# One-pass products read and write backwards, with token tiles at sixteen starting places

## The chip, the cores and the metric

The kernel runs on one core of a Trainium2 chip. The metric is the device time of one execution in microseconds. The median of three runs stands for a kernel, and one more execution is profiled.

## What is computed

The reference is a trunk of two layers for 512 tokens of width 1024, in float32. Tokens are mixed by differential attention in the first layer and by chunked gated linear attention in the second; in both, four heads attend to 256 memory tokens beside it. One input projection feeds all heads, one output projection takes their joined results, and a gated MLP with a causal convolution of width 3 follows. Cut to its skeleton:

```
for i in range(2):
    h = rms_norm(x, attn_norm[i])
    proj = h @ w_in                                  # one input projection
    mix = diff_attention(proj) if i == 0 else gla_attention(proj)
    cross = memory_cross_attention(proj, mem)        # 4 heads, 256 memory tokens
    x = x + concatenate([mix, cross]) @ w_out[i]
    h = rms_norm(x, ffn_norm[i])
    u = causal_conv(h @ w_up[i]) + conv_b[i]
    a, g = split(u)
    x = x + (silu(g) * a) @ w_down[i]
```

Nearly all of the arithmetic is in the products with `w_in`, `w_mem_kv`, `w_out`, `w_up` and `w_down`.

## The kernel before

The residual stream is kept transposed: eight tiles `xT[k]` of 128 features by 512 tokens. Two such tiles share one buffer of 4096 bytes a partition (`x2`, sixteen buffers); `pair` and `split_tiles` hand out the two halves, and `load_x` takes whole buffers.

A float32 product is made of three products in the type float32r, which TensorE runs in one pass. Each operand is split in a rounded part and the rest, `hi` on ScalarE (lines 227, 263, 306) and `lo` on VectorE (lines 230, 265, 309), and hi x hi, hi x lo and lo x hi are summed in PSUM. These are the one-pass products of the change. They stand at four places:

- `gemm` (lines 327 to 329): the input and memory projections. The stationary operand is a block of 128 tokens of an `x2` tile, the moving operand a slice of weights with 512, 272 or 256 columns.
- the first projection (line 507), of the same kind, while the inputs still arrive.
- `product` (lines 348 to 350): the output and up projections. Here the weights are stationary and the moving operand is a tile of 512 tokens.
- `down` (line 1173): the down projection, worked as a scheme of half-size blocks with fewer products. The weights are stationary and the moving operand is a block of 256 tokens, in an `x2` tile or in `midh` and `midl`, which are not of `x2`.

Attention, the transposes (`transpose`, line 196) and the sums of squares use float32, which takes several passes; they are not touched.

Weights come as blocks of 512 KB by DMA from the SP queue into six raw buffers and are split into five buffers of `whi` and five of `wlo`. The order on TensorE is that in which the program is written. In the attention layers a queue of work (`Filler`) puts a few microseconds of projection between steps of attention, and its costs and fill times are fixed numbers in the code. In the MLP each group of up projections is followed by its `down`.

Where tiles lie matters to this change. As allocated, every tile that a one-pass product of the change reads starts at 416 modulo 512 bytes: all `x2`, `whi`, `wlo`, `midh`, `midl` and the tiles of the mixers' results. Stationary slices step by 512 bytes, moving ones by 512, 1024 or 2048, so both operands of a product start at the same place modulo 512. The exception is the projection with 272 columns, whose weight slices step by 1088 bytes and start at 416, 480 and 32.

Of the kernel before, what the change touches and what calls it, by code (L numbers as in the profile page):

```python
# [11 lines left out]
F32 = mybir.dt.float32  # L12
# [9 lines left out]
S = 512  # L22
KT = D // 128
# [8 lines left out]
X2, XS, EM = 16, 5, 7  # L32
# [118 lines left out]
def trunk(ctx, tc, head_d, x_t, mem_t, wpack, cols_a_d, cols_d, conv_d, gate_d, rel_bias, diff_lambda, consts, onehot, out):  # L151
    nc = tc.nc
    mm = nc.tensor.matmul
# [3 lines left out]
    xs = ctx.enter_context(tc.tile_pool(name="xs", bufs=1))  # L157
# [6 lines left out]
    def bank(tag):  # L164
        return ps.tile([128, 512], F32, name=f"ps_{tag}", tag=tag)

    def xtile():
        return xs.tile([128, S], F32, name="xt", tag="xs", bufs=XS)

    def pair(dt=F32):  # L170
        t = xs.tile([128, 2, S], dt, name="x2", tag="x2", bufs=X2)
        return t[:, 0], t[:, 1]

    def split_tiles(pool=None, tag=None, bufs=None):
# [8 lines left out]
    def blk(b, w=128):  # L183
        return slice(w * b, w * b + w)
# [5 lines left out]
    ones = C[:, 640:768]  # L190
    eps = perm.tile([128, 1], F32, name="eps")
    V.memset(eps, EPS)

    def transpose(dst, src):
        n = src.shape[0]
        nc.tensor.transpose(dst, src, ident[:n, :n])  # L196
# [117 lines left out]
    def gemm(sh, sl, nb, key, w, evac, hook=None, order=None, hold=1):  # L314
        got, open_, held = [], {}, []
        order = order or [(b, "mm") for b in range(nb)]

        def unit(b, tag, k0, k1):
            if not got:
                for x in key if isinstance(key, list) else [key]:  # L320
                    got.extend(weights(x))
            if k0 == 0:
                open_[b] = bank(tag)[:, :w]
            p = open_[b]
            for k in range(k0, k1):
                hi, lo = got[k]
                mm(p, sh[k][:, blk(b)], hi, start=k == 0, stop=False)  # L327
                mm(p, sh[k][:, blk(b)], lo, start=False, stop=False)  # L328
                mm(p, sl[k][:, blk(b)], hi, start=False, stop=k == KT - 1)  # L329
            if k1 == KT:  # L330
                held.append(b)
                if len(held) < hold:
                    return
                if hook is not None and order[hold - 1][0] == b:
                    hook()
                for x in [x for x in held if x in open_]:
                    evac(x, open_.pop(x))
        for b, tag in order:
            for k in range(0, KT, 2):
                F.add(6 * w / 2370.0, lambda b=b, tag=tag, k=k: unit(b, tag, k, k + 2))  # L340


    def product(p, parts, n, pairs, ids=None):
        ids = range(len(parts)) if ids is None else ids
        first, last = (ids[0], ids[-1]) if len(ids) == len(parts) else (0, len(parts) - 1)
        for i in ids:
            (hi, lo), (bh, bl) = parts[i], pairs[i]
            mm(p, hi[:, blk(n)], bh, start=i == first, stop=False)  # L348
            mm(p, hi[:, blk(n)], bl, start=False, stop=False)  # L349
            mm(p, lo[:, blk(n)], bh, start=False, stop=i == last)  # L350


    xT, xpair = [None] * KT, [None] * (KT // 2)
# [56 lines left out]
    first = [bank("mm"), bank("mm"), bank("sm"), bank("sm")]  # L410
# [24 lines left out]
    with tc.tile_pool(name="ini", bufs=1) as ip, tc.manual_schedule(engines={E.Activation, E.DVE, E.Pool, E.SP}):  # L435
        idle = ip.tile([128, 512], F32, name="idle")
        rb = ip.tile([32, 6], F32, name="rb")
        oh = ip.tile([32, 640], F32, name="oh")
        bs = pair()
        bs = bs[0][:6], bs[1][:6, :128]  # L440
        lv = xtile()[:, :256]
        G.memset(idle, 0.0)
        p = bank("tp")
        for n in (512, 320):
            mm(p[:, :n], idle[:, 0:128], idle[:, :n], start=True, stop=True)


        raws = [ip.tile([128, WTILE], F32, name=f"raw{i}") for i in range(4)]
        A.dma_start(raws[0][:, blk(0, S)], wpack[0, :, blk(0, S)])
        head = ip.tile([128, 32 + S], F32, name="head")  # L450
        for c in (slice(0, 32 + S // 2), slice(32 + S // 2, 32 + S)):
            load(head[:, c], head_d[:, c])
        xT[0] = head[:, 32:]
        for k in range(1, KT):
            if k % 2:
                two = pair()
            xT[k] = two[1 - k % 2]
            load(xT[k], x_t[k])
            load(raws[k // 2][:, blk(k % 2, S)], wpack[k // 2, :, blk(k % 2, S)])
        load(cols_a, cols_a_d)  # L460
        at[0] = 4
        load(C[:, 640:768], consts[:, 640:768])
        load(rb, rel_bias)
        load(oh, onehot)
        second = [load_raw(raw_tile(), WTILE) for _ in range(3)]
        load(cols, cols_d)
        load(lv, diff_lambda[0].rearrange("a b -> (a b)").partition_broadcast(128))
        parts, acc, split_w = [], [None], [None]
        made.append(parts)

        def operands(k):
            if k % 2 == 0:
                split_w[0] = [wp.tile([128, WTILE], F32R, name=n, tag=n, bufs=WB) for n in ("whi", "wlo")]
            c = blk(k % 2, S)
            hi, lo = split_w[0]
            xh[k], xl[k] = split_tiles()
            if k == 0:
                V.tensor_copy(hi[:, c], raws[0][:, c])
                V.tensor_sub(lo[:, c], raws[0][:, c], hi[:, c].bitcast(F32))
                for t in (blk(0, S // 2), blk(1, S // 2)):  # L480
                    split(xh[0][:, t], xl[0][:, t], xT[0][:, t], col(0, head))
            else:
                split(xh[k], xl[k], xT[k], col(k, head))
                split_weights(c, raws[k // 2], hi, lo)
            parts.append((hi[:, c], lo[:, c]))
            squares(xT[k], acc)

        operands(0)
        for k in range(KT):
            if k + 1 < KT:  # L490
                operands(k + 1)
            if k == 0:
                second.append(load_raw(raws[0], WTILE))
            if k == 4:
                bias_rows(rb, oh, bs)
            if k == KT - 2:
                make_piece(second, lambda: token_rsqrt("lg", acc[0], NB, r_x[:, 0]))
                weights(("qk", 0))
                small_vectors()
                for c in range(2):  # L500
                    load(bias_d[:, 512 * c:min(512 * c + 512, 640)], bs[c])
            hi, lo = parts[k]
            terms = (xh[k], hi), (xh[k], lo), (xl[k], hi)
            todo = [(b, i) for b in range(NB) for i in range(3)]
            for b, i in sorted(todo, key=lambda bi: bi[1]) if k == 0 else todo:
                xp, w = terms[i]
                mm(first[b], xp[:, blk(b)], w, start=k == 0 and i == 0, stop=k == KT - 1 and i == 2)

    load(C[:, 0:640], consts[:, 0:640])
    for i in range(4):  # L510
# [545 lines left out]
    def load_x(src):  # L1056
        for k in range(KT):
            if k % 2 == 0:
                xpair[k // 2] = xs.tile([128, 2, S], F32, name="x2", tag="x2", bufs=X2)
            xT[k] = xpair[k // 2][:, k % 2]  # L1060
            nc.sync.dma_start(xT[k], src[k])

# [43 lines left out]
    def ffn(pool, l, acc):  # L1106
# [47 lines left out]
        def down(g, mids, finish):  # L1154
            last, ks = len(mids) - 1, tuple(range(len(mids)))
            parts, banks, first, last_group = {}, {}, used[0], g + 1 == len(GROUPS)

            def step(c, tag, w, m, ks=ks, start=False, more=True):
                if (c, w) not in parts:
                    parts[c, w] = weights(("d", l, g, c, w), more)  # L1160
                elif more:
                    prefetch(first + more)
                if start:
                    banks[c, tag] = bank(tag)
                p = banks[c, tag]
                hi, lo = parts[c, w]
                for k in ks:
                    mh, ml = mids[k][m]
                    for n in range(2):
                        o, ws = p[:, blk(n, 256)], slice(256 * k + 128 * n, 256 * k + 128 * n + 128)  # L1170
                        terms = (hi, mh), (hi, ml), (lo, mh)
                        for i, (a, b) in enumerate(terms):
                            mm(o, a[:, ws], b, start=start and (k, n, i) == (0, 0, 0), stop=k == last and i == 2,  # L1173
                               skip_group_check=True)

            def add(c, tag, f, t):
# [91 lines left out]
        for what, i in _ffn():  # L1268
            if what == "up":
# [12 lines left out]
                if i % 2 == 0:  # L1282
                    w = pool.tile([128, 8, 256], F32, name="w", bufs=1)
# [3 lines left out]
            else:  # L1287
                n, last = GROUPS[i], i == len(GROUPS) - 1
# [93 lines left out]
```

## Time and profile before

| | |
|---|---|
| median of 3 runs | 1171.81 us (1171.26 to 1171.84) |
| the profiled execution | 1170.8 us |
| its span, from first to last instruction | 1168.9 us |
| granted TensorE clock | 1.000 |
| TensorE busy | 1155.8 us, 99% of the span |
| VectorE busy | 886.6 us, 76% |
| ScalarE busy | 599.2 us, 51% |
| DMA | 117.94 MB, mean 101 GB/s |

In the profile PE is TensorE, PEld its loads of stationary operands (which lie beside its products), DVE is VectorE and ACT ScalarE. A product's row shows its length from start to finish; successive products overlap, so the time that each takes from the next is the distance between their starts.

### The profile page before, as it was taken

To read this page: it belongs to the slowest core of one execution; us is meant where nothing else is said; L and a number is where in the kernel's file an instruction comes from. 1 tells how busy PE (TensorE), PEld (TensorE's weight loads), DVE (VectorE), ACT (ScalarE), POOL (GpSimd) and SP (SyncE) were. 2 spreads that over 40 slices of the span, in tenths; PEclk is the share of its full clock that TensorE was granted. 3 is DMA by queue.
4 is the path that set the end of the run, shared out by engine and by line. 5 is a ranking of instruction groups with operands and counts; after the bars stand their busy time and mean duration, and the time that the engine had idled before them with its cause. 6 is when DMAs were issued, how large, how long until landed. Compare 5 with 4: busy or idle time off the path is not lost.

```text
span 1168.9 us, 16705 instructions
## 1 busy us (share of the span) xinstructions
PE 1155.8 (99%) x6448; PEld 988.7 (85%) x6448; DVE 886.6 (76%) x1454; ACT 599.2 (51%) x1048; POOL 4.1 (0%) x17
## 2 busy tenths in 40 slices
PE   9999999999999999999999999999999999999998
PEld 6887777788898889988998788988889988998888
DVE  7747687679886778668897746868998677876885
ACT  6856677566444444344467534536654344434441
POOL 0000000000000000000000000000000000000000
PEclk9999999999999999999999999999999999999999
DMA  9432213143225222522253221144221632253212
GB/s 313 162 97 90 68 55 127 59 129 97 64 70 182 91 73 72 162 93 70 66 169 112 73 73 46 55 153 126 86 68 64 189 99 73 72 155 98 72 37 73
DMA packets 39853, 117.94 MB, mean 101 GB/s; under 512 B 4735, under 2 KB 7608, under 8 KB 39774
## 3 DMA queue, kind: packets, MB, share of 16 engines
q1 hardware_dynamic: 39630, 116.62, 31.7%
q8 instruction: 51, 0.84, 0.3%
q14 instruction: 28, 0.23, 0.1%
q10 hardware_dynamic: 144, 0.26, 0.1%
HBM read 112.65 MB, written 4.21 MB: 100 GB/s over the span
## 4 chain that ended last, share of the span: by engine, by line
PE 91%; DVE 6%; ACT 2%; issue 1%; DMA 0%; DVEq 0%; ACTq 0%
PE ps_lg L1173 10%; PE ps_mm L348 9%; PE ps_mm L349 9%; PE ps_mm L350 9%; PE ps_sm L350 7%; PE ps_sm L348 7%; PE ps_sm L349 7%; PE ps_mm L327 5%; PE ps_mm L329 5%; PE ps_mm L328 5%; PE ps_tp L1173 5%; PE ps_mm L1173 3%; PE ps_tp L196 2%; PE ps_lg L686 1%; PE ps_sm L722 1%; DVE wlo L230 1%
## 5 line engine op out<-in xcount | busy, mean ns | idle before, releaser
L230 DVE TENSOR_TENSOR wlo<-raw,whi 128x1024 fp32r<-128x1024 f32 (+4 forms) x164 | 186.5, 1140 | 86.5 <-ACT whi L227 85.7
L227 ACT CAST whi<-raw 128x1024 fp32r<-128x1024 f32 (+4 forms) x164 | 160.7, 985 | 155.6 <-PE ps_sm L349 69.9
L348 PE MATMUL ps_mm<-x,whi 128*128 128x512 f32 x438 | 172.6, 394 | 0.3 <-DVE midh L1264 0.3
L349 PE MATMUL ps_mm<-x,whi 128*128 128x512 f32 x438 | 170.6, 389 | 0.2 <-DVE x L309 0.2
L350 PE MATMUL ps_mm<-x,wlo 128*128 128x512 f32 x438 | 170.6, 390 | 0.0
L348 PE MATMUL ps_sm<-x,whi 128*128 128x512 f32 x378 | 148.0, 392 | 0.0
L349 PE MATMUL ps_sm<-x,whi 128*128 128x512 f32 x378 | 147.1, 389 | 0.0
L350 PE MATMUL ps_sm<-x,wlo 128*128 128x512 f32 x378 | 147.1, 389 | 0.0
L327 PE MATMUL ps_mm<-whi,x 128*128 128x512 f32 (+2 forms) x336 | 132.0, 393 | 0.0
L329 PE MATMUL ps_mm<-whi,x 128*128 128x512 f32 (+2 forms) x336 | 126.6, 377 | 0.5 <-DVE x L309 0.4
L328 PE MATMUL ps_mm<-wlo,x 128*128 128x512 f32 (+2 forms) x336 | 125.9, 375 | 0.0
L263 ACT CAST whi<-raw 128x1024 fp32r<-128x1024 f32 (+1 forms) x60 | 58.3, 978 | 86.7 <-PE ps_sm L349 26.2
L348 PEld LDWEIGHTS ps_mm<-x,whi 128*128 128x128 f32 x438 | 82.3, 188 | 17.4 <-issue 0.9
L350 PEld LDWEIGHTS ps_mm<-x,wlo 128*128 128x128 f32 x438 | 82.2, 188 | 17.1
L349 PEld LDWEIGHTS ps_mm<-x,whi 128*128 128x128 f32 x438 | 82.3, 188 | 17.0 <-DVE x L309 0.6
L265 DVE TENSOR_TENSOR wlo<-raw,whi 128x1024 fp32r<-128x1024 f32 (+1 forms) x60 | 67.9, 1131 | 25.2 <-ACT whi L263 25.1
L349 PEld LDWEIGHTS ps_sm<-x,whi 128*128 128x128 f32 x378 | 71.0, 188 | 15.1 <-issue 0.5
L348 PEld LDWEIGHTS ps_sm<-x,whi 128*128 128x128 f32 x378 | 71.0, 188 | 15.0 <-issue 0.5
L350 PEld LDWEIGHTS ps_sm<-x,wlo 128*128 128x128 f32 x378 | 70.9, 188 | 14.8
L1173 PE MATMUL ps_lg<-midh,whi 128*128 128x256 f32 x264 | 75.0, 284 | 1.8 <-DVE x L1178 1.8
L1173 PE MATMUL ps_lg<-midl,whi 128*128 128x256 f32 x264 | 74.7, 283 | 0.0
L1173 PE MATMUL ps_lg<-midh,wlo 128*128 128x256 f32 x264 | 74.7, 283 | 0.0
(308 smaller groups left out, 2287.2 us busy)
## 6 DMA issues: line engine op xcount, KB each, us to landing
raw<-in_wpack_dram SPq DMA_DIRECT2D x170, 512.0 KB, 3.6
raw<-in_wpack_dram SPq DMA_DIRECT2D x24, 384.0 KB, 3.1
x<-in_x_t_dram SPq DMA_DIRECT2D x15, 256.0 KB, 5.2
xres<-x SPq DMA_DIRECT2D x8, 256.0 KB, 3.7
x<-xres SPq DMA_DIRECT2D x8, 256.0 KB, 5.1
raw<-in_wpack_dram SPq DMA_DIRECT2D x7, 256.0 KB, 5.4
bt<-bias_d SPq DMA_DIRECT2D x6, 256.0 KB, 4.9
x<-in_mem_t_dram SPq DMA_DIRECT2D x4, 256.0 KB, 6.1
```

The lines of the kernel that those rows point to most:

```text
L196: nc.tensor.transpose(dst, src, ident[:n, :n])
L227: ins = A.copy(hi[:, c], raw[:, c])
L230: V.tensor_sub(lo[:, c], raw[:, c], hi[:, c].bitcast(F32))
L263: A.copy(hi[:, c], raw[:, c])
L265: todo = [lambda: V.tensor_sub(lo[:, c], raw[:, c], hi[:, c].bitcast(F32)), lambda: [sum_weights((*key[:3], *x)) for x in after]]
L327: mm(p, sh[k][:, blk(b)], hi, start=k == 0, stop=False)
L328: mm(p, sh[k][:, blk(b)], lo, start=False, stop=False)
L329: mm(p, sl[k][:, blk(b)], hi, start=False, stop=k == KT - 1)
L348: mm(p, hi[:, blk(n)], bh, start=i == first, stop=False)
L349: mm(p, hi[:, blk(n)], bl, start=False, stop=False)
L350: mm(p, lo[:, blk(n)], bh, start=False, stop=i == last)
L1173: mm(o, a[:, ws], b, start=start and (k, n, i) == (0, 0, 0), stop=k == last and i == 2, skip_group_check=True)
```

## The change

Two things change together. A buffer of `x2` gets 32 bytes more, so the sixteen buffers, which lie one behind the other, start at sixteen places modulo 512 bytes, 32 apart (416, 448, 480, 0, 32 and so on to 384). And at the four places above, the moving operand and the output are given with step -1 along the columns, so the columns pass through TensorE in the reverse order and land where they landed before. Stationary operands are read as before, and the weight tiles and `midh`, `midl` start where they did. The four small products of line 885 stay forward.

```diff
+    def two_tiles(dt=F32):
+        t = xs.tile([128, 2 * S + 8], dt, name="x2", tag="x2", bufs=X2)
+        return t[:, :2 * S].rearrange("p (a b) -> p a b", a=2)
+
     def pair(dt=F32):
-        t = xs.tile([128, 2, S], dt, name="x2", tag="x2", bufs=X2)
+        t = two_tiles(dt)
         return t[:, 0], t[:, 1]
...
+    def back(t):
+        return t[:, ::-1]
...
-                mm(p, sh[k][:, blk(b)], hi, start=k == 0, stop=False)
-                mm(p, sh[k][:, blk(b)], lo, start=False, stop=False)
-                mm(p, sl[k][:, blk(b)], hi, start=False, stop=k == KT - 1)
+                mm(back(p), sh[k][:, blk(b)], back(hi), start=k == 0, stop=False)
+                mm(back(p), sh[k][:, blk(b)], back(lo), start=False, stop=False)
+                mm(back(p), sl[k][:, blk(b)], back(hi), start=False, stop=k == KT - 1)
...
-            mm(p, hi[:, blk(n)], bh, start=i == first, stop=False)
-            mm(p, hi[:, blk(n)], bl, start=False, stop=False)
-            mm(p, lo[:, blk(n)], bh, start=False, stop=i == last)
+            mm(back(p), hi[:, blk(n)], back(bh), start=i == first, stop=False)
+            mm(back(p), hi[:, blk(n)], back(bl), start=False, stop=False)
+            mm(back(p), lo[:, blk(n)], back(bh), start=False, stop=i == last)
...
-                mm(first[b], xp[:, blk(b)], w, start=k == 0 and i == 0, stop=k == KT - 1 and i == 2)
+                mm(back(first[b]), xp[:, blk(b)], back(w), start=k == 0 and i == 0, stop=k == KT - 1 and i == 2)
...
-                xpair[k // 2] = xs.tile([128, 2, S], F32, name="x2", tag="x2", bufs=X2)
+                xpair[k // 2] = two_tiles()
...
-                            mm(o, a[:, ws], b, start=start and (k, n, i) == (0, 0, 0), stop=k == last and i == 2,
+                            mm(back(o), a[:, ws], back(b), start=start and (k, n, i) == (0, 0, 0), stop=k == last and i == 2,
                                skip_group_check=True)
```

The order of the instructions stays the same on every engine. What the built program has besides is a wait of TensorE for its own semaphore (`PE_49`) on some first products of an accumulation. 71 of its rows name such a wait, where 55 did. One of the places is in the first layer's output projection, beside attention's products. TensorE's rows there before:

```order
L686 MATMUL ps_lg<-kT,qT 128x128 x2
L722 MATMUL ps_sm<-v_388,em 128x128 [waits Activation_49]
L722 MATMUL ps_sm<-v_388,em 128x128 x3
L348 MATMUL ps_mm<-x_1240,whi 128x512
L349 MATMUL ps_mm<-x_1240,whi 128x512
```

And with the change, where the lines of the file are 7 further down:

```order
L693 MATMUL ps_lg<-kT,qT 128x128 x2
L729 MATMUL ps_sm<-v_388,em 128x128 [waits Activation_49]
L729 MATMUL ps_sm<-v_388,em 128x128 x3
L355 MATMUL ps_mm<-x_1240,whi 128x512 [waits PE_49]
L356 MATMUL ps_mm<-x_1240,whi 128x512
```

The first product of the output projection's sum now waits for an earlier product of TensorE; nothing has changed places.

## The prediction

> **What bounds the kernel now.** I read the clock first, then the busy times and the chain of waits, then TensorE's own waits.
>
> ```profile
> core 0: 1168.9 us, clock 1.000
> PE 1155.8 (99%) x6448; PEld 988.7 (85%) x6448; DVE 886.6 (76%) x1454; ACT 599.2 (51%) x1048; POOL 4.1 (0%) x17
> PE 91%; DVE 6%; ACT 2%; issue 1%; DMA 0%; DVEq 0%; ACTq 0%
> ```
> ```profile
> PE ps_lg L1173 <- DVE x L1178: 1.8, 2, 0.9
> ...
> PE ps_mm L349 <- DVE x L309: 0.2, 1, 0.2
> ```
>
> The clock is full, TensorE is busy for 99% of the span and holds 91% of the chain, and the longest of its twelve kinds of wait adds up to 1.8 us. So the time is what TensorE takes per product times the number of products. "Busy" hides the interesting part, since products overlap (one is shown as 0.39 us long and the next starts before it ends). What counts is the distance from start to start, which the timeline of TensorE gives for 512 columns, and the merged pieces of the chain for 256:
>
> ```profile
> 399.74 0.39 PE L348 MATMUL ps_mm<-x,whi 128*128 128x512 f32 x1
> 399.96 0.39 PE L349 MATMUL ps_mm<-x,whi 128*128 128x512 f32 x1
> ...
> 402.46 0.39 PE L348 MATMUL ps_mm<-x,whi 128*128 128x512 f32 x1
> ```
> ```profile
> 463.93 8.64 PE ps_lg L1173 x72
> ```
>
> Twelve products from 399.74 to 402.46 are 226.7 ns each; 72 products in 8.64 us are 120.0 ns each. The difference of 106.7 ns for 256 columns is 0.4167 ns a column, and 226.7 - 512 x 0.4167 = 13.3 ns is left over, the same 13.3 at 256 columns (120.0 - 106.7). Every one-pass product pays these 13.3 ns besides its columns.
>
> Is that the price of changing the weights? The four-pass float32 products and the transposes change them just as often (timeline pieces, with the mean length of one from the groups by line):
>
> ```profile
> 704.66 0.81 PE L1000 MATMUL ps_sm<-gv,x 128*128 128x192 f32 x4
> L1000 PE MATMUL ps_sm<-gv,x x32: 323/324/328, 704.7 to 776.9; 128*128 128x192 f32 x32
> 151.53 1.03 PE L196 MATMUL ps_tp<-C,em 128*128 128x128 f32 x8
> L196 PE MATMUL ps_tp<-C,em 128*128 128x128 f32 x92 | 14.0, 273 | 0.0
> ```
>
> Start to start is (0.81 - 0.324)/3 = 162 ns at 192 columns and (1.03 - 0.273)/7 = 108 ns at 128: 0.84 ns a column, twice the one-pass figure, and about 2 ns left over. So a change of weights costs about 2 ns where the moving operand is read at half the speed, and 13.3 where it is read at full speed. That looks like a full-speed stream held up by something that a half-speed stream absorbs, and what runs beside every product is the load of the next weights. Two more places of the timeline say that the 13.3 is not rigid. First the products with 272 columns, whose moving operands begin at three places modulo 512 bytes, while in all other one-pass products of the kernel before both operands begin at one and the same place (so the tiles are allocated); then 512 columns in a stretch broken up by float32 work:
>
> ```profile
> 611.59 0.29 PE L327 MATMUL ps_mm<-whi,x 128*128 128x272 f32 x1
> ...
> 614.23 0.29 PE L327 MATMUL ps_mm<-whi,x 128*128 128x272 f32 x1
> ```
> ```profile
> 149.69 0.39 PE L328 MATMUL ps_mm<-wlo,x 128*128 128x512 f32 x1
> ...
> 150.84 0.39 PE L327 MATMUL ps_mm<-whi,x 128*128 128x512 f32 x1
> 151.08 0.39 PE L328 MATMUL ps_mm<-wlo,x 128*128 128x512 f32 x1
> 151.30 0.39 PE L329 MATMUL ps_mm<-whi,x 128*128 128x512 f32 x1
> ```
>
> The 21 products from 611.59 to 614.23 take 125.7 ns, 12.4 over their columns. The seven from 149.69 to 151.30 take 230 ns, and single ones 240 and 220 (the view rounds to 10 ns): the left-over moves between about 7 and 27 ns, with the same instructions. I read that as a hold-up that depends on how the two reads, of the moving operand and of the next weights, lie to each other.
>
> **The change part by part.** *Direction.* The number of products reversed comes from the windows over the whole span for lines 348 (349 and 350 are its twins), 327 (328 and 329 likewise), 507 and 1173, in this order, with the forms of 327:
>
> ```profile
> 0.00:1168.90 1168.90, 326.81 (x832) 156.23 (x832) 1.00 0.32 101
> 0.00:1168.90 1168.90, 136.69 (x352) 66.30 (x352) 1.00 0.32 101
> 0.00:1168.90 1168.90, 22.78 (x96) 17.90 (x96) 1.00 0.32 101
> 0.00:1168.90 1168.90, 223.59 (x1848) 222.75 (x1848) 1.00 0.32 101
> ```
> ```profile
> L327 PE MATMUL ps_mm<-whi,x 128*128 128x512 f32 x288 | 117.8, 409 | 0.0
> L327 PE MATMUL ps_mm<-whi,x 128*128 128x256 f32 x32 | 9.6, 301 | 0.0
> ```
>
> 3 x 832 + 3 x 352 + 96 + 1848 = 5496 products. 3456 of them have 512 columns, 3 x 32 + 1848 = 1944 have 256, and the other 96 have 272. Their left-overs are 5496 x 13.3 ns = 73 us, 6% of the span, nearly all on the path. How fast the two reads pass each other follows from the loads:
>
> ```profile
> L348 PEld LDWEIGHTS ps_mm<-x,whi 128*128 128x128 f32 x438 | 82.3, 188 | 17.4 <-issue 0.9
> ...
> L619 PEld LDWEIGHTS ps_tp<-em,vm 128*64 128x64 f32 x64 | 3.4, 136 | 1.6 <-ACT em L711 0.8 <-issue 0.5 <-ACT rs_y L217 0.3
> ```
>
> 64 columns more take 52 ns more, so a load reads its 512 bytes in about 104 ns, in which the moving operand advances by about 1024. Read in the same direction, the two places shift by 512 bytes against each other during a load: they stay close for a long time, and a stream that is held up stays close longer. Read in opposite directions they shift by 1536. If nearness counts modulo 512 bytes, that is three meetings in place of one, each a third as long, and perhaps short enough for a buffer to absorb part of it. The gain lies between nothing (the same time spent in meetings, no buffer) and all but the 2 ns of the float32 rows: 5496 x 11.3 = 62 us. For 256 columns the limit is the same, since loads follow one another in 108 ns at line 196, 12 below the 120. No row shows a product read backwards, so I take the middle, 5.65 ns each or 31 us. With TensorE's 91% of the chain that is 28 us.
>
> The trace has one read against the address order, on VectorE: line 691 reads `bt` with step -1. Its longest (512 columns) stands beside a forward sum of the same size, line 1178:
>
> ```profile
> L691 DVE CUSTOM_DVE_ANT_0 em<-ps_lg,bt x48: 278/485/693, 44.0 to 219.4; 128x128 f32<-128x128 f32 x12, 128x256 f32<-128x256 f32 x12, 128x384 f32<-128x384 f32 x12, 128x512 f32<-128x512 f32 x12
> L1178 DVE TENSOR_TENSOR x<-x,ps_lg x48: 674/680/689, 334.2 to 1165.0; 128x512 f32<-128x512 f32 x48
> ```
>
> 693 against 689 ns: backwards costs that engine nothing. For TensorE, and for writing PSUM backwards, there is no row; the cost of that at worst is the third rival.
>
> *Starting places.* With sixteen places, the pair of reads meets in a different phase from product to product. The bounds are the spread seen above: 220 to 240 ns for 512 columns, -7 to +13 around 226.7, with a mean of 230 where it was unsettled. In the reversed kernel I count it at nothing, as the reads pass through every phase three times in a load anyway. For VectorE, ScalarE and the DMAs the new places cost nothing that would show: at 15 ns more (the spread of line 1178) for each of VectorE's 1454 instructions, 22 us would meet 282 us of idle time.
>
> *Added waits.* No instruction moves on any engine; 16 more of TensorE's wait for TensorE's own semaphore (71 for 55 before). In the list of waits above, TensorE never waits for itself, so such a wait is normally long met; at worst it drains the product ahead, 0.39 - 0.227 = 0.163 us, 16 times: 2.6 us. I take half, 1.3. Behind it stand only TensorE's next products.
>
> *What is late next.* VectorE, in the feed-forward stages:
>
> ```profile
> 250.00:331.00 81.00, 81.00 (x357) 66.71 (x356) 75.02 (x106) 43.83 (x61) 0.00 (x0) 1.00 0.30 90
> 347.00:442.00 95.00, 94.95 (x479) 81.21 (x479) 70.64 (x88) 41.07 (x51) 0.00 (x0) 1.00 0.37 117
> ```
>
> It is busy 75.02 of 81 us (93%) in the first, 74% in the second. With 5.65 of 226.7 ns (2.5%) gone from TensorE's time it fills 95% of the first and still fits; at the full 5% TensorE would begin to wait for it.
>
> Sum: 1168.9 - 28 + 1.3 = 1142 for the span. The median of the runs, 1171.81, lies 2.9 above the profiled span (that execution itself took 1170.8), so 1145.
>
> **The rivals.** *It changes nothing* (0.12): the 13.3 ns belong to the one-pass product itself, whatever its direction. For it: exactly 13.3 at both 256 and 512 columns, on every tile. Against it: 12.4 at 272 columns, and 220 to 240 ns in the unsettled stretch. Time 1172, within 0.2% (2.3 us, about what a measurement of this kernel can tell from no change). The Trainium skill states this side in "TensorE: Matmul & The Clock Gate", Step-by-step: moving operand and weight load have independent read ports, so a load takes no bandwidth from the running product. By that rule reversing cannot help, and the time stays 1172; the unsettled rows speak against it. The same page's back-to-back gap leaves about 2.5 ns per product over its columns, where this trace has 13.3, so its rule does not tell what these rows contain.
>
> *The places unsettle it* (0.18): the settled 226.7 is lost for phases like those of the stretch at 150 us, and reversal buys nothing. At the 230 ns found there, 3456 x 3.3 ns = 11 us: 1183. At 236 it would be 32 us: 1204. It decides as soon as the mean distance of 512-column products exceeds 226.7. For it: this is the only disorder that the trace shows, and its mean is worse. Against it: it comes with forward reading.
>
> *Backwards is half speed* (0.10): reading or writing against the address order streams a column in 0.84 ns as in the float32 rows. The columns are 3456 x 512 + 1944 x 256 + 96 x 272 = 2.29 million, x 0.42 ns = 960 us more: about 2130. Against it: line 691. For it stands only a rule of the Trainium skill, "PSUM — Partial Sum Buffer", Specifications: any access pattern that is not contiguous slows products significantly, as lines are 8 bytes. Whether step -1 counts as that, no run here shows.
>
> **How the numbers follow.** Forecast (the hold-up shrinks) 0.60, nothing 0.12, places 0.18, half speed 0.10. The low end is the full gain, 62 x 0.91 = 56 us: 1115, and 3 for a forecast whose waits shrink too: 1112. The high end takes in the case of no change and the nearer half of the places' range: 1188. What lies outside is most of half speed and the far part of the places. Faster by over 0.2%: 0.60; within: 0.10; slower: 0.30, the two slower rivals and a little of "nothing".
>
> **What would show it.** Right: products of 512 columns start every 215 to 224 ns and those of 256 every 109 to 118, with more waits of TensorE for VectorE around line 1178 and for `wlo`. Wrong: exactly 226.7 and 120.0 (nothing), a mean of 228 to 236 for 512 columns (places), or over 300 (half speed). A shorter distance with an unchanged span would say that VectorE took over.

## The result, and the profile after

| | before | after |
|---|---|---|
| median | 1171.53 us (1170.9 to 1171.84) | 1189.1 us (1188.97 to 1189.36) |
| ratio, 95% interval | | 1.0149 (1.0137 to 1.0161) |
| profiled span | 1168.9 us | 1187.5 us |

The change makes the kernel 1.5% slower. The page of the kernel after, in the places that were read first (cores, busy times, chain by engine), then the longest of TensorE's waits:

```profile
core 0: 1187.5 us, clock 1.000
PE 1174.6 (99%) x6448; PEld 987.4 (83%) x6448; DVE 887.4 (75%) x1454; ACT 598.6 (50%) x1048; POOL 4.1 (0%) x17
PE 88%; DVE 8%; ACT 2%; issue 1%; DMA 1%; DVEq 0%; ACTq 0%
```
```profile
PE ps_lg L1180 <- DVE x L1185: 2.4, 4, 1.0
...
PE ps_mm L356 <- DVE x L316: 0.2, 1, 0.2
```

The clock is full again, VectorE and ScalarE are busy within 0.8 us of before, TensorE 18.8 us longer; its longest kind of wait went from 1.8 to 2.4 us. No engine and no wait took over: the products themselves start further apart. TensorE's timeline in the same place of the up projection, and the chain in the same down projection:

```profile
400.03 0.40 PE L355 MATMUL ps_sm<-x,whi 128*128 128x512 f32 x1
400.27 0.40 PE L356 MATMUL ps_sm<-x,whi 128*128 128x512 f32 x1
...
404.24 0.40 PE L355 MATMUL ps_mm<-x,whi 128*128 128x512 f32 x1
```
```profile
472.63 8.52 PE ps_lg L1180 x72
```

Eighteen products from 400.03 to 404.24 are 233.9 ns each, where it was 226.7; 72 products in 8.52 us are 118.3 ns each, where it was 120.0. So 512 columns lost about 7 ns a product and 256 columns won 1.7 (the view rounds starts to 10 ns). The distance from each product's start to the next, summed over the whole trace by the place in the program (waits included, worked out from the starts of all rows), gives the account:

| us | up and output projections (348 to 350) | input and memory projections (327 to 329, 512 columns) | first projection (507) | down (1173) | all other products |
|---|---|---|---|---|---|
| before | 570.8 | 204.8 | 22.4 | 224.3 | 141.0 |
| after | 587.0 | 208.3 | 23.7 | 222.3 | 140.6 |
| difference | +16.2 | +3.5 | +1.3 | -2.0 | -0.4 |

The sum is +18.6 us, and the span grew by 18.6. The 2496 products of the first column at 6.7 ns would be 16.7 us; nearly all of the loss is there. Of the 1.3 us at the first projection some 0.5 are the products themselves. The rest are pauses between them, and these differ by themselves: the same place took 23.2 us in a later run (only the down projection backwards) that changes nothing there.

### The profile page after: what moved, and what is told of

It is laid out like the page before. It is cut to its first block, busy times and chain, and to the rows that moved or that the text cites. A ratio compares the mean times of both kernels' runs of the same rounds, so it can differ in the third digit from the quotient of the medians.

```text
span 1187.5 us, 16711 instructions
## 1 busy us (share of the span) xinstructions
PE 1174.6 (99%) x6448; PEld 987.4 (83%) x6448; DVE 887.4 (75%) x1454; ACT 598.6 (50%) x1048; POOL 4.1 (0%) x17
## 4 chain that ended last, share of the span: by engine, by line
PE 88%; DVE 8%; ACT 2%; issue 1%; DMA 1%; DVEq 0%; ACTq 0%
PE ps_mm L356 9%; PE ps_mm L355 9%; PE ps_mm L357 9%; PE ps_lg L1180 8%; PE ps_sm L357 8%; PE ps_sm L356 8%; PE ps_sm L355 8%; PE ps_mm L334 5%; PE ps_mm L336 5%; PE ps_mm L335 5%; PE ps_tp L1180 4%; PE ps_mm L1180 2%; PE ps_tp L203 2%; PE ps_lg L693 1%; PE ps_sm L729 1%; DVE wlo L272 1%
## 5 line engine op out<-in xcount | busy, mean ns | idle before, releaser
L355 PE MATMUL ps_mm<-x,whi 128*128 128x512 f32 x438 | 175.9, 402 | 0.1
L356 PE MATMUL ps_mm<-x,whi 128*128 128x512 f32 x438 | 174.1, 397 | 0.2 <-DVE x L316 0.2
L357 PE MATMUL ps_mm<-x,wlo 128*128 128x512 f32 x438 | 174.0, 397 | 0.0
L355 PE MATMUL ps_sm<-x,whi 128*128 128x512 f32 x378 | 151.1, 400 | 0.0
L357 PE MATMUL ps_sm<-x,wlo 128*128 128x512 f32 x378 | 150.2, 397 | 0.0
L356 PE MATMUL ps_sm<-x,whi 128*128 128x512 f32 x378 | 150.1, 397 | 0.0
L334 PE MATMUL ps_mm<-whi,x 128*128 128x512 f32 (+2 forms) x336 | 133.6, 398 | 0.0
L336 PE MATMUL ps_mm<-whi,x 128*128 128x512 f32 (+2 forms) x336 | 128.2, 382 | 0.5 <-DVE x L316 0.4
L355 PEld LDWEIGHTS ps_mm<-x,whi 128*128 128x128 f32 x438 | 82.4, 188 | 19.9 <-issue 0.6
L357 PEld LDWEIGHTS ps_sm<-x,wlo 128*128 128x128 f32 x378 | 71.0, 188 | 17.2
L336 PEld LDWEIGHTS ps_mm<-whi,x 128*128 128x128 f32 x336 | 63.1, 188 | 14.1 <-DVE x L316 1.0
L334 PEld LDWEIGHTS ps_mm<-whi,x 128*128 128x128 f32 x336 | 63.3, 188 | 13.9 <-issue 2.8
```

The lines of the kernel that those rows point to most:

```text
L334: mm(back(p), sh[k][:, blk(b)], back(hi), start=k == 0, stop=False)
L336: mm(back(p), sl[k][:, blk(b)], back(hi), start=False, stop=k == KT - 1)
L355: mm(back(p), hi[:, blk(n)], back(bh), start=i == first, stop=False)
L356: mm(back(p), hi[:, blk(n)], back(bl), start=False, stop=False)
L357: mm(back(p), lo[:, blk(n)], back(bh), start=False, stop=i == last)
```

## The experiments

The theories that were to be told apart: (1) reading backwards itself makes 512 columns slower; (2) the sixteen places unsettle the products; (3) writing PSUM backwards costs; (4) the added waits cost.

### Each half alone, and reading backwards without writing backwards

Three kernels, each with one edit against the kernel after (the third on top of the second). Places alone, forward:

```diff
     def back(t):
-        return t[:, ::-1]
+        return t
```

> The sixteen starting places alone; every product reads and writes forward again. Theory A (the reversed direction costs the time, the places nearly nothing): products of 512 columns at 226.7 to 230 ns and the time at 1171 to 1180 us. Theory B (the places unsettle the two reads, the direction is innocent): 512 columns at about 233.5 ns as with both parts, and 1186 to 1191 us.

Direction alone, all tiles at 416 modulo 512 again:

```diff
-        t = xs.tile([128, 2 * S + 8], dt, name="x2", tag="x2", bufs=X2)
+        t = xs.tile([128, 2 * S], dt, name="x2", tag="x2", bufs=X2)
```

> The reversed direction alone; the token tiles start at one place again. Theory A: 512 columns near 233.5 ns, 256 columns near 118.5, and 1186 to 1191 us, as with both parts. Theory B: 512 columns at 226.7 or below, and 1160 to 1173 us.

Direction alone with forward outputs, at all four places:

```diff
-                mm(back(p), sh[k][:, blk(b)], back(hi), start=k == 0, stop=False)
+                mm(p, sh[k][:, blk(b)], back(hi), start=k == 0, stop=False)
```

> One place for all tiles, the moving operand read backwards, the output written forwards, so that the columns of every one-pass product land in reversed order and the values are other ones. Theory A1 (reading backwards is what costs): 512 columns near 233.5 ns and a time near 1189 us. Theory A2 (writing PSUM backwards is what costs): 512 columns at 226.7 or below and at most 1172 us. Theory B: as A2.

Measured: places alone 1187.17 us, ratio 1.0137 (1.012 to 1.0154); direction alone 1188.43, ratio 1.0147 (1.0131 to 1.0162); backwards reading with forward outputs 1188.01 in its one execution. Timeline of places alone, then the chain of direction alone, in the same up projection:

```profile
400.14 0.41 PE L356 MATMUL ps_mm<-x,whi 128*128 128x512 f32 x1
400.38 0.39 PE L357 MATMUL ps_mm<-x,wlo 128*128 128x512 f32 x1
...
404.10 0.39 PE L355 MATMUL ps_mm<-x,whi 128*128 128x512 f32 x1
```
```profile
400.36 0.23 PE ps_sm L355
401.06 0.23 PE ps_mm L355
...
407.36 0.23 PE ps_mm L355
```

With the places alone, 17 products take 232.9 ns each, single ones between 220 and 240 as the view rounds them. With direction alone, line 355 comes every third product: from 400.36 to 407.36 are thirty products, 233.3 ns each, and they are even. Either half by itself takes away the 226.7 ns and costs nearly what both cost together: +15.9 and +17.1 us against +17.6. The halves do not add.

The third kernel bears on (3) and (4). With forward outputs the time stays, and the built program has 55 rows that name a wait for `PE_49`, as before the change, where direction alone has 71: the 16 waits came with the reversed outputs. 1188.4 against 1188.0 leaves them and the writing together some 0.4 us, which a single execution cannot tell from nothing.

### One product at a time, with the other engines idle

The kernel before with series of 16 products appended, each series alone on TensorE. `write` and `read` of -1 reverse the output or the moving operand, `n` is the number of columns, `at` shifts the moving operand's place; the calls are left out here.

```diff
+        def series(name, n, write=1, read=1, at=0, cols=128, count=16):
+            p = ps.tile([128, 512], F32, name="ps_" + name, tag=next(tags))
+            for i in range(count):
+                o, m = p[:cols, :n], M[:, at:at + n]
+                mm(o if write > 0 else o[:, ::-1], W[:, 128 * (i % 8):128 * (i % 8) + cols],
+                   m if read > 0 else m[:, ::-1], start=i == 0, stop=i == count - 1)
```

> The kernel before, followed by series of 16 one-pass products each while the other engines are idle: 512, 448, 384, 320 and 256 columns, forward, with both reversed, with only the output reversed and with only the moving operand reversed; then stationary operands of 96, 64 and 32 columns; then sixteen starting places of the moving operand in each direction. The whole is about 130 us longer. Theory A (a reversed stream costs per column, and less is lost during the load): forward leaves 13.3 ns at every length, reversed rises from about 12 ns at 256 columns to 20 at 512, by 0.033 ns a column; A1 has this in the series with the reversed read, A2 in those with the reversed write. Theory B: at one and the same place forward and reversed series are alike within 1 ns, and the series over the places spread over 220 to 240 ns. If the 13.3 ns stand for the load, forward products with 64 stationary columns leave half of it.

The chain of waits; each row is a series of 16, in us. In order: 512 columns with both reversed, output only, moving operand only; 256 columns forward and both reversed; stationary operands of 64 and 32 columns; moving operand 0, 32, 64 and 256 bytes further on, forward, and 0 and 64 bytes reversed:

```profile
1173.94 3.74 PE ps_both L1321 x16
1177.67 3.65 PE ps_wback L1321 x16
1181.32 3.74 PE ps_rback L1321 x16
...
1218.83 1.92 PE ps_fwd L1321 x16
1220.76 1.90 PE ps_both L1321 x16
...
1233.95 3.69 PE ps_fwdc64k L1321 x16
...
1241.37 3.71 PE ps_fwdc32k L1321 x16
...
1248.82 3.64 PE ps_fwdp0b L1321 x16
1252.46 3.74 PE ps_fwdp32b L1321 x16
1256.20 3.67 PE ps_fwdp64b L1321 x16
...
1278.52 3.63 PE ps_fwdp256b L1321 x16
...
1308.22 3.74 PE ps_bothp0b L1321 x16
...
1315.69 3.73 PE ps_bothp64b L1321 x16
```

A row holds the first few products too, which are longer: forward at 0 bytes they start 236, 233 and 230 ns apart and then settle at 226.7. What follows goes by the distances of the last products of each series, less 0.4167 ns a column.

- *Direction.* At 512 columns the left-over is 13.3 ns forward, 13.3 with the output reversed, 19.9 with the moving operand reversed, 20.0 with both. At 256 columns both reversed give 11.7. These are the 233 and 118 ns of the kernel after, with VectorE and ScalarE silent and DMA too, but for a few fetches of instructions: nothing beside TensorE is needed for it. Reading backwards is what costs, writing backwards costs nothing. The Trainium skill says in "PSUM — Partial Sum Buffer", Specifications, that an access pattern that is not contiguous slows products significantly; for step -1 the 226.7 ns of the series with only its output reversed speak against it.
- *Length.* Reversed against forward: 20.0 against 13.3 at 512 columns, 20.1 against 16.4 at 448, 17.2 against 13.4 at 384, even at 320 (13.3), and better only at 256. Forward, too, 13.3 does not hold at every length: the later run under "What sits beside what" has 16.3 to 16.8 at 480, 496, 504 and 508 columns.
- *Place.* Forward, as the moving operand goes on by 32 bytes each time: 13.3, 20, 15.7, 20, 20, 20.7, 20, 20, and then the same again. Reversed, 20 at every place. So the 13.3 of the kernel before is a value that holds forward, with the two operands at one place modulo 256 bytes; its tiles, all at 416 modulo 512, stood there.
- *Load.* With stationary operands of 64 and 32 columns the loads do get shorter, 135 and 108 ns where 128 columns take 188. The left-over of the products does not: it goes from 13.3 to about 16 and 18.3.

### A map of the places

The same series for eight places of the moving and eight of the stationary operand (given in bytes), and finer shifts:

```diff
+        for st in range(0, 256, 32):
+            for mv in range(0, 256, 32):
+                series(f"m{mv}bw{st}b", (mv,), st)
```

> The kernel before, followed by series of 16 forward one-pass products of 512 columns while the other engines are idle: every pair of eight starting places of the moving and eight of the stationary operand, 32 bytes apart; then shifts of 4 to 28 bytes of the one, the other and both; then moving operands that alternate between two places; then always the same weights, and the weights in descending order. Theory C (what settles a stream at 13.3 ns is the distance of the two operands modulo 256 bytes): equal shifts of both stay at 226.7 ns, and the map repeats along its diagonal; 32 bytes apart gives 233, 64 gives 229 as in the earlier series. Theory D (the place of the moving operand alone counts): the map depends on the moving place only, and a shift of both by 32 bytes gives 233. Theory E (the weights' place alone counts beside it in no way, each pair has its own value): neither. Either way the best of the 64 says whether any place is better than the 226.7 ns of the kernel before.

The chain, moving operand (m) and stationary operand (w) shifted by so many bytes:

```profile
1179.03 3.63 PE ps_s_m0bw0b L1321 x16
1182.66 3.74 PE ps_s_m32bw0b L1321 x16
1186.39 3.67 PE ps_s_m64bw0b L1321 x16
...
1208.71 3.72 PE ps_s_m0bw32b L1321 x16
1212.44 3.63 PE ps_s_m32bw32b L1321 x16
```

Either operand alone moved by 32 bytes takes the series from 3.63 to over 3.7 us, both together bring it back. All 64 places follow the distance of moving from stationary operand modulo 256: 0 gives 13.3 ns, 64 gives 15.7, the others 18.5 to 20.8. A shift of both by 16 bytes, though, gives 20.0, so the place within 32 bytes counts as well. Of the moving operand's shifts below 32 bytes, 28 keeps 13.3 and 4 gives 23.4. A series that keeps one stationary slice, and one that takes the slices downwards, stay at 13.3. A moving operand that alternates between 0 and 32 bytes leaves 16.7, halfway between the 13.3 and 20.0 of the two places: alternating as such adds nothing.

### A constant distance in the whole kernel

If the distance decides, a kernel forward in all, with the `x2` tiles 64 bytes off the weights, must be slower. In the up and output projections the moving operand is then 64 bytes ahead, 2 ns or so by the map; in the input, memory and first projections, where the weights are the moving operand, it is 64 behind, up to 6.7 ns. Two pads, on the kernel before:

```diff
+    for pool, n in ((xs, 16), (wp, 48)):
+        G0.memset(pool.tile([128, n], F32, name="pad", tag="pad", bufs=1), 0.0)
```

> The kernel before, all forward, with the token tiles moved 64 bytes against the weight tiles (by two small tiles that nothing else uses). Theory C (the distance of the two operands modulo 256 bytes sets the left-over, as in the map): lines 348 to 350 have the moving operand 64 bytes ahead and go to 229 ns, lines 327 to 329 and 507 have it 64 behind and go to 233, so 2496 x 2.3 + 960 x 4.5 to 6.7 = 10 to 12 us more: 1181 to 1184 us. The rival, that a mixture of places within the kernel is what hurts and one common shift is harmless: 1171 to 1173 us.

Measured 1185.34 us, ratio 1.0118 (1.0104 to 1.0132), a little above the range. Two stretches of the up projections of the first layer:

```profile
299.82 0.39 PE L353 MATMUL ps_sm<-x,wlo 128*128 128x512 f32 x1
...
303.94 0.39 PE L353 MATMUL ps_mm<-x,wlo 128*128 128x512 f32 x1
```
```profile
399.82 0.40 PE L351 MATMUL ps_mm<-x,whi 128*128 128x512 f32 x1
...
404.02 0.40 PE L351 MATMUL ps_mm<-x,whi 128*128 128x512 f32 x1
```

Eighteen products take 228.9 ns each in the first, as in the map, and 233.3 in the second. Between the two stands the layer's first down projection (336 to 366 us). In both layers the up projections ahead of the first down projection settle at about 229 ns and all those behind it at 233.3, though their operands lie 64 bytes apart throughout. So a shift of 64 bytes in the allocation, with no other change, costs most of what the change costs, and one distance in bytes can have two steady values; that was not foreseen. What of the stages before or beside them picks the value was not tried.

### Only the down projection backwards

What of the change wins time, taken alone:

```diff
-                            mm(o, a[:, ws], b, start=start and (k, n, i) == (0, 0, 0), stop=k == last and i == 2,
+                            mm(o[:, ::-1], a[:, ws], b[:, ::-1], start=start and (k, n, i) == (0, 0, 0), stop=k == last and i == 2,
```

> The kernel before, with the read and the write reversed in the down projection alone (line 1173, 1848 products of 256 columns), everything else forward and all tiles at one place. Theory C with the measured distances of reversed products at 256 columns: 118.5 for 120.0 ns there, 226.7 at 512 columns as before, so 1848 x 1.5 = 2.8 us less: 1168 to 1169.5 us. If VectorE's sums after each step (line 1178) take the place of what TensorE gains, or the reversed products of 256 columns owe their gain to something else: 1171 us or more.

Measured 1169.24 us, ratio 0.9981 (0.9972 to 0.999), 2.1 us less and within the range that was expected. The chain in a down projection:

```profile
464.15 8.52 PE ps_lg L1173 x72
```

It is the 118.3 ns of the kernel after, while 512 columns keep their 226.7.

### What sits beside what, and 256 columns

Two questions: is it the product's own stationary operand or that of the next load whose distance counts, and what do places do at 256 columns? Series in which both operands alternate between two places, in step (`in`) or against each other (`anti`), and eight places at 256 columns, forward (`f`) and reversed (`r`):

```diff
+        for d in (32, 64, 96):
+            series(f"in{d}b", (0, d), (0, d))
+            series(f"anti{d}b", (0, d), (d, 0))
+        for mv in range(0, 256, 32):
+            series(f"f256m{mv}b", (mv,), n=256)
```

> The kernel before, followed by series of 24 one-pass products with the other engines idle. First the moving and the stationary operand both alternate between two places 32, 64 or 96 bytes apart: once so that each product has its own two operands at one place and the next weights at another, once so that each has the next weights at its own place and its own weights at the other. If the load of the next weights, beside the product, is what holds the stream up, the second kind stays at 226.7 ns and the first goes to 229 to 234; if the product's own weights count, the reverse. Then 256 columns, forward and reversed, at eight distances; then 288, 480, 496, 504 and 508 columns. Forward at 256 columns is expected at 120.0 for distance 0 and the reversed near 118.5 for all.

The chain, 24 products a row:

```profile
1185.69 5.58 PE ps_s_in32b L1322 x24
1191.27 5.52 PE ps_s_anti32b L1322 x24
...
1219.05 2.88 PE ps_s_f256m0b L1322 x24
...
1236.13 2.73 PE ps_s_f256m192b L1322 x24
...
1241.69 2.84 PE ps_s_r256m0b L1322 x24
```

The first question stays open: if one of the two loads decided, either `in` or `anti` would stand at 13.3, and at 32 bytes they stand at 18.4 and 16.7. For 256 columns one place stands out: with the moving operand 192 bytes ahead, products settle at 113.3 ns, a left-over of 6.6 ns, the least that any series showed. Forward at 0 it is 120.0, and the reversed series at 0 has 11.7 left over. But most other forward places also leave 11.1 to 11.8, and reversed the left-over is 13.3 at 64 and 128 bytes. So the 1.7 ns that reversing wins at 256 columns holds for operands at one place, and moving an operand wins as much.

### Using it: the `mid` tiles 192 bytes ahead

On the kernel before, a pad moves `midh` and `midl`, which only the down projection reads as moving operands:

```diff
+        G.memset(pool.tile([128, 48], F32, name="pad", bufs=1), 0.0)
```

> The kernel before, all forward, with the tiles midh and midl 192 bytes further on (by one small tile ahead of them), so that 1320 of the 1848 products of the down projection have the moving operand 192 bytes ahead of the weights modulo 256; all other products stay at distance 0. Theory C: those 1320 go from 120.0 to 113.3 ns as in the series of 256 columns at 192 bytes, 8.8 us less, 1162 to 1164 us. If the series' 113.3 needs idle engines or one fixed pair of tiles: 118 ns and 1168 us, or no change.

Measured 1165.69 us, ratio 0.9951 (0.9938 to 0.9965): faster than both kernels, though by 5.7 us and not the 8.8 that were expected. Chain, and TensorE's longest wait:

```profile
463.61 8.32 PE ps_lg L1174 x72
...
477.53 2.72 PE ps_mm L1174 x24
```
```profile
PE ps_lg L1174 <- DVE x L1179: 3.5, 4, 1.2
```

The products on `mid` tiles run at 2.72 us for 24, 113.3 ns each. Products on `x2` tiles, which did not move, stay near 120. Worked out from all starts, the products on `mid` tiles are 8.0 us shorter in sum without their pauses, and the pauses ahead of them took 2.3 us back: the waits for VectorE ahead of the first product on a `mid` tile grew by 1.7 us.

Reversing just those too, since they win 1.7 ns that way:

```diff
-                            mm(o, a[:, ws], b, start=start and (k, n, i) == (0, 0, 0), stop=k == last and i == 2,
+                            mm(*((o[:, ::-1], a[:, ws], b[:, ::-1]) if m in ("t1", "b11") else (o, a[:, ws], b)), start=start and (k, n, i) == (0, 0, 0), stop=k == last and i == 2,
```

> As the run with midh and midl 192 bytes further on, and the other 528 products of the down projection, whose moving operand lies in the token tiles, read and written backwards. Theory C: 528 x 1.5 = 0.8 us below that run, 1161 to 1163 us. If VectorE's sums set the pace of these steps: no difference.

This missed: 1168.36 us, ratio 0.9974 (0.9965 to 0.9984). Nearly half of the gain was lost, and lost where nothing had been changed, in the products on `mid` tiles:

```profile
478.31 2.83 PE ps_mm L1174 x24
```

They are forward and 192 bytes ahead as in the kernel without the reversal, and start 117.8 ns apart, which is also what a series under "Finer places" settles at. Their place alone does not fix their distance. Of the 62 groups of products on `mid` tiles in a kernel (one output in a row), 57 settle at 113.3 ns without the reversal and 54 at 117.8 with it; each kernel has a few of the other kind.

### Finer places

> The kernel before, followed by series of 20 forward products of 512 columns with the other engines idle, the moving operand 0 to 252 bytes ahead of the weights in steps of 4, then both together 8, 16 and 24 bytes further at eight distances, then 256 columns at 184 to 204 bytes. Theory C in its simple form (only the distance counts): the shifted sets repeat the first one at multiples of 32. From the earlier series with both operands 16 bytes further (233 ns instead of 226.7) I expect that they don't, and that the place modulo 32 counts as well. If some distance leaves less than 13.3 ns at 512 columns, the kernel before can be bettered there too; I expect none below 226.

Sixty-four distances 4 bytes apart at 512 columns, three sets with both operands shifted by 8, 16 and 24 bytes, and 256 columns around 192. Chain, 20 products a row:

```profile
1185.34 4.53 PE ps_s_m0b L1321 x20
...
1301.36 4.78 PE ps_s_m100b L1321 x20
...
1521.14 4.62 PE ps_s_m0bw16b L1321 x20
1530.43 4.54 PE ps_s_m64bw16b L1321 x20
...
1600.21 2.36 PE ps_s_k256m192b L1321 x20
```

At 512 columns no place is below 13.3 ns; some (0, 28, 60, 108, 156, 252) reach it, the worst (100, 120, 132, 196, 244) are at 26.7. With both operands 16 bytes further, the distances 64, 160 and 224 reach 13.3 and 0 does not (17.8, where the map had 20.0 for the same products). And at 256 columns and 192 bytes the series settled at 117.8 ns here, where the same series gave 113.3 beside the alternating ones: the same products at the same distance have two steady values. The two series follow different ones and write to different PSUM buffers; what picks the value was not found.

## Why the prediction was wrong, point by point

- *The bound held.* The time is TensorE's distance from start to start: the distances account for all 18.6 us of the span.
- *The step that failed is "so I take the middle, 5.65 ns each or 31 us".* Its direction was wrong where it weighed most. Reading backwards gave +6.7 ns in place of -5.65 at 512 columns and -1.7 at 256. By place in the program that is +16.2, +3.5 and +1.3 us against -2.0. Its bounds were set from "nothing" to a full gain, and the text gave no reason that excluded a loss: the trace of before showed a stretch with a mean of 230 ns, so the range of the term should have reached above 226.7 as well. (The single products of 220 and 240 ns that the prediction reads there come from starts rounded to 10 ns; unrounded they lie between 224 and 235.)
- *The picture under it failed too.* It read 13.3 ns as a hold-up by the next load of weights, and that as something above a floor of 2 ns. That the two operands' places act on each other is right: the series show it with every other engine idle. But 13.3 was the best value that any place gave at 512 columns, not a typical one. The kernel before stood there with all its tiles, by the way it was allocated. And loads of a quarter of the columns gave a larger left-over, not a smaller one, so the sum over meetings during a load has nothing to stand on. What is met instead, the runs do not show.
- *The float32 rows were no floor.* That float32 products leave 2 ns was read as what a one-pass product could reach. The least that any one-pass series reached was 6.6, at 256 columns and one place.
- *Places counted at nothing in the reversed kernel:* this held. Reversed, the left-over at 512 columns is 20 at every place that was tried, and the kernel after differs from direction alone by 1189.1 against 1188.4 us. It held for want of anything to lose, though: forward, the same places cost 15.9 us.
- *The added waits, 1.3 us between 0 and 2.6:* the runs with and without them lie some 0.4 us apart, inside the bounds; no row of TensorE's waits names TensorE.
- *VectorE late next* was not put to the test, since TensorE became slower. Where it became faster by 5.7 us, its longest wait for VectorE grew from 1.8 to 3.5 us, so the direction was right.
- *The rivals.* "It changes nothing" is out, by 17.6 us. "Backwards is half speed" is out: 233.3 ns where it would be over 300. "The places unsettle it" came nearest, with 228 to 236 ns as its sign and 1183 to 1204 as its times. Of its two parts the first is shown (places alone: 1187.2), the second is not: it has reversal buy nothing, and reversal alone costs as much. That the change consists of two losses, which do not add, was in no case that the prediction listed. The Trainium skill's rule that the prediction put on the side of "nothing" ("TensorE: Matmul & The Clock Gate", Step-by-step) has the two reads in ports of their own, without a price between them. The map, in which moving either operand by 32 bytes costs 6.7 ns and moving both costs nothing, does not agree with it as far as the time of a product goes.

## What to carry to other kernels

Before a cost is called removable, ask whether the kernel may already stand at its best value: compare the settled figure with the disturbed ones, and if the disturbed ones are worse, bound the term on that side first. When products run back to back, the starting places of the moving and the stationary operand are part of the kernel: write them down modulo 256 bytes before changing a tile's size, padding or order, since 64 bytes of allocation cost 14 us here and 192 bytes on other tiles won 5.7. Then measure in the kernel itself, since a series by itself did not always give the kernel's value. Try halves of a double change alone; here each half costs nearly all of it.

## What the hardware showed that was not expected

- One-pass products with 512 columns and full stationary operands have left-overs from 13.3 to 26.7 ns as the places of the two operands and the direction of reading vary, with the other engines idle.
- With both operands at one place, reading the moving operand backwards costs 6.7 ns at 512 columns, nothing at 320, and wins 1.7 at 256; its left-over of 20 ns at 512 does not depend on the place in steps of 32 bytes. Writing PSUM backwards costs nothing (226.7 ns).
- One distance in bytes can have two steady values: 113.3 and 117.8 ns with 256 columns and the moving operand 192 bytes ahead, 228.9 and 233.3 ns with 512 columns and 64 bytes ahead. The first pair went with the reversal of other products (57 of 62 groups at 113.3 without it, 54 of 62 at 117.8 with it), the second with the down projection in between. So what a run of products goes through first may matter; no run shows this by itself.
- Why the distance counts modulo 256 bytes, why a common shift of 16 bytes counts, and whether it is the product's own stationary operand or the next load that is met, stays open.
